# Running maxima sent as rows through DRAM, the causal mask added by GpSimd, and the gate rows turned by transposes

## The chip, the cores and the metric

The kernel runs on one core of one Trainium2 chip. A core has five engines that work side by side and meet only at semaphores: TensorE for matmuls (PE in the profile, its weight loads apart as PEld), VectorE (DVE), ScalarE (ACT), GpSimd (POOL) and SyncE (SP), which here issues every DMA from one queue, in order. Matmuls write to PSUM, eight banks of 128 x 512 floats; everything else is in SBUF, the on-chip memory with 128 partitions, or in DRAM. The metric is the device time of one execution in microseconds (us); lower is better.

## The reference, cut to what matters

The reference is one layer of a streaming encoder over 2048 tokens of 1024 features. One input projection feeds a banded attention of eight heads and an mLSTM of four heads of 128 features; gated outputs of both are projected and added to the input, and a feed-forward part of width 4096 follows, with a final norm. What the change touches is the mLSTM. For each head it has an input gate `i` and a forget gate `f` per token, both linear in the normed input, and it is computed in chunks:

```
logf = log_sigmoid(f);  bcum = cumsum(logf) within the chunk
dmat[t, s] = bcum[t] - bcum[s] + i[s]        where s <= t, else -inf
m_t = max(bcum[t] + m_st, max_s dmat[t, s])  running maximum
dw  = exp(dmat - m_t)
qk  = (q . k) * dw
num = exp(g - m_t) * (C q) + qk v;   den = exp(g - m_t) * (n . q) + sum(qk)
h   = num / max(|den|, exp(-m_t))
```

With `u[s] = i[s] - bcum[s]` and `mt` the running maximum of `u` (with the state's maximum), the weight is `dw = exp(u[s] - mt[t])`: a number per token `s`, on a partition, less a number per token `t`, along the row, and 0 where `s` is after `t`.

## The kernel before, in words

The 2048 tokens are four blocks (b = 0 to 3) of T = 512. Blocks 0 and 1 are projected one after the other with three-part matmuls (each operand is split into a rounded part and a remainder, and three products are added). Blocks 2 and 3 form a span whose products go through a scheme with seven products in place of eight over halves of the features and the two blocks: the operand list `X` holds seven sets of four tiles. Set 0 is the first half of block 2's features, set 1 its second half, set 2 the sum of both halves of block 3, set 5 the first half of block 2 less that of block 3, set 6 the second half of block 3. The feed-forward part uses the same scheme, with spans (0, 1) and (2, 3); its inner results `u` go through DRAM and come back through a ring of eight tiles.

The code is written as generators. `Flow` runs them on a clock of its own: each `yield` names an engine and a cost, gets buffers from a pool or a PSUM bank, or waits for an event. After that `Order` takes the instructions so made and lists them again for every engine by estimated lengths, transfer times and due times; the order on an engine is then fixed, and so is the one of the DMAs on SP's queue. A change in pool sizes, in costs or in instructions can thus move others too.

The mLSTM of a block runs in these steps:

- **Gate sums.** PE multiplies the gate weights `gw` (128 x 40 for each of eight feature tiles: 8 columns rounded, zeros, and at column 32 their 8 remainders) with the two parts of the normed block, 512 tokens as columns: in `dense` (L803) for blocks 0 and 1, 16 matmuls each, and in `gates_in` (L1495) for blocks 2 and 3. Block 2 takes sets 0 and 1, 16 matmuls. Block 3 takes set 0 with the first weights and set 6 with the second in one bank, and set 5 with the first weights in a second bank, 24 matmuls; the difference of the banks is its first half plus its second.
- **`gates`.** ACT copies the 40 rows (L1461), for block 3 DVE subtracts the second bank (L1464), four matmuls with a selecting matrix `sel` (L1468) put tokens on partitions and add the remainders' rows, and DVE adds the biases (block 0 scales by its norm too).
- **`gates_rest`.** A chain of small operations on 128 x 16 tiles (four chunks of 128 tokens by four heads) makes `u`, `mt` and the exponentials `ex`. At its end four transposes (L1587) bring `mt` into rows, 4 heads x 512 tokens; ACT copies them (L1589) into `mtt` and DVE writes the remainders below (L1592). Then the event `gates` is set.
- **`rec_head`**, once for each head: PE writes the mask into a bank by a bf16 matmul of an identity with `maskb` (L1670), and adds `-mt` of the head in all rows by a matmul of a selecting column of `nsel` with `mtt` (L1671). ACT takes the exponential of the four chunks with `u` as bias (L1675) into the tile `w`. PE transposes `k` (L1682) and multiplies `k` and `q` (L1693), DVE multiplies that by `w` (L1695), and the products with the values and the state follow (L1707 to L1709). Two heads at most are held at a time; `load_rec` brings their `q`, `k` and values (L1625, L1630) back from DRAM. The final transposes are L1742, and the result is stored to `mix` in DRAM and read again by `take_mix` ahead of the projection.

Weights are read into four `wraw` tiles, split by ACT (L583) and DVE (L585) into three `wsp` tiles, and used by PE. Attention (L1388, L1415, L1446) and the mLSTM of blocks 0 and 1 lie among their input projections; those of blocks 2 and 3 among the second half of the first span's feed-forward part (L644 to L646).

Of the kernel before, what the change touches and what calls it, by code (L numbers as in the profile page):

```python
# [36 lines left out]
KT = D // P  # L37
AH, AD = 8, 64
MH = 4
FF = 4096  # L40
EPS = 1e-6
NEG = -1e30
# [330 lines left out]
class Layer:  # L373
# [8 lines left out]
    def make_tiles(self, pool, psum):  # L382
        nc = self.nc
        f32 = lambda name, *shape: pool.tile([P, *shape], F32, name=name)
        f32r = lambda name, *shape: pool.tile([P, *shape], F32R, name=name)
        self.wsplit = Pool([f32r(f"wsp{i}", 2, 1024) for i in range(3)])
        self.wraw = Pool([f32(f"wraw{i}", 1024) for i in range(4)])
        self.rpool = Pool([f32r(f"r{i}", 2, T) for i in range(28)])
        self.bias = Pool([f32(f"bias{i}", 640) for i in range(2)])
        self.sc = Pool([(f32(f"sc{i}", 640), f32(f"scs{i}", 4)) for i in range(4)])  # L390
        self.temp = Pool([f32(f"tmp{i}", 516) for i in range(6)])
        self.ctx = Pool([f32(f"ctx{i}", 516) for i in range(16)])
        self.banks = Banks([psum.tile([P, 512], F32, name=f"bank{i}") for i in range(8)])
# [4 lines left out]
        self.identb = pool.tile([P, P], BF16, name="identb")  # L398
        self.maskb = pool.tile([P, 1, P], BF16, name="maskb")
        self.gw = f32r("gw", KT, 40)  # L400
        self.sel = f32("sel", 8)
# [7 lines left out]
        self.mtt = f32r("mtt", T)  # L409
        self.nsel = f32r("nsel", 8)  # L410
# [12 lines left out]
        self.fmid = [f32(f"mie{i}", NT) for i in range(NB)]  # L423
# [13 lines left out]
    def setup_late(self):  # L437
# [7 lines left out]
        zero = raw[:, 64:384]  # L445
        nc.vector.memset(zero, 0.0)
        nc.vector.tensor_copy(self.gw.rearrange("p a b -> p (a b)"), zero)
        nc.vector.tensor_copy(self.gw[:, :, 0:8], gwr)
        nc.vector.tensor_sub(self.gw[:, :, 32:40], gwr, self.gw[:, :, 0:8].bitcast(F32))
        nc.vector.memset(raw[:, :512], 0.0)  # L450
        nc.vector.tensor_copy(self.mtt, raw[:, :512])
        fl.put(self.temp, raw)
        yield "sp", 300, 2200
        nc.sync.dma_start(self.sel, io["sel"])
# [6 lines left out]
        nc.vector.tensor_copy(self.identb, self.ident)  # L461
        nc.vector.tensor_scalar(self.maskb[:, 0], self.tri, 1.0, -NEG, op0=ALU.subtract, op1=ALU.mult)
        nc.vector.tensor_scalar(self.nsel, self.sel, -1.0, None, op0=ALU.mult)
# [321 lines left out]
    def dense(self):  # L785
        fl = self.fl
        none = [None] * KT
        for b in range(2):
# [11 lines left out]
            for k in range(KT):  # L800
                yield "pe", 433
                for j in range(2):
                    self.nc.tensor.matmul(bk[:40], self.gw[:, k], vs[k][:, j],  # L803
                                          start=k == 0 and j == 0, stop=k == KT - 1 and j == 1)
# [651 lines left out]
    def gates(self, b, bk, less=None):  # L1456
        fl, nc, B, sm = self.fl, self.nc, self.blk[b], self.sm
        V = nc.vector
        (tmp,) = yield "get", self.temp, 1
        yield "act", act_ns(512, True)  # L1460
        nc.scalar.copy(tmp[:40, :512], bk[:40])  # L1461
        if less is not None:
            yield "dve", dve_ns(512)
            V.tensor_sub(tmp[:40, :512], tmp[:40, :512], less[:40])  # L1464
            fl.put(self.banks, less)
        yield "pe", 756
        for c in range(NT):
            nc.tensor.matmul(bk[:, c * 8:c * 8 + 8], tmp[:40, c * P:(c + 1) * P], self.sel[:40],  # L1468
                             start=True, stop=True)
        gf = self.gf[b % 2]  # L1470
        if b == 0:
            for c in range(NT):
                yield "dve", 85
                V.scalar_tensor_tensor(gf[:, c], bk[:, c * 8:c * 8 + 8], self.rr["x"][:, c:c + 1],
                                       self.bif[:, c], op0=ALU.mult, op1=ALU.add)
        else:
            yield "dve", 85
            V.tensor_add(gf, bk[:, :32].rearrange("p (a b) -> p a b", a=NT), self.bif)
        fl.put(self.temp, tmp)
        fl.put(self.banks, bk)  # L1480
        fl.set(B["gf"])

    def gates_in(self, A, aev):

        fl = self.fl
        for b, use in ((2, (((0, 0), (1, 4)),)), (3, (((0, 0), (6, 4)), ((5, 0),)))):
            bks = []
            for part in use:
                bks += (yield "get", self.banks, 1)
                for x, (m, k0) in enumerate(part):  # L1490
                    for k in range(4):
                        yield "wait", [aev[m][k]]
                        yield "pe", 433
                        for j in range(2):
                            self.nc.tensor.matmul(bks[-1][:40], self.gw[:, k0 + k], A[m][k][:, j],  # L1495
                                                  start=x == k == j == 0,
                                                  stop=x == len(part) - 1 and k == 3 and j == 1)
            fl.spawn(self.gates(b, *bks), 1)

    def gates_rest(self, b):  # L1500
# [84 lines left out]
        yield "pe", 428  # L1585
        for c in range(NT):
            nc.tensor.transpose(bk[:MH, c * P:(c + 1) * P], sm["mt"][:, c * MH:(c + 1) * MH], self.ident)  # L1587
        yield "act", act_ns(512, True)
        nc.scalar.copy(self.mtt[:MH], bk[:MH])  # L1589
        yield "dve", dve_ns(512)  # L1590
        yield "dve", 85
        V.tensor_sub(self.mtt[32:32 + MH], bk[:MH], self.mtt[:MH].bitcast(F32))  # L1592
        fl.put(self.banks, bk)
        fl.set(B["gates"])

    def recurrence_far(self, b):
# [3 lines left out]
        for h in range(MH):  # L1600
# [7 lines left out]
            fl.spawn(self.load_rec(b, h), 1)  # L1608
            fl.spawn(self.rec_head(b, h), 1)
# [5 lines left out]
    def load_rec(self, b, h):  # L1615
# [14 lines left out]
        fl.set(B["mvh_ev"][h])  # L1630

# [30 lines left out]
    def rec_head(self, b, h):  # L1662
# [5 lines left out]
        (bk,) = yield "get", self.banks, 1  # L1668
        yield "pe", 440
        mm(bk.rearrange("p (c t) -> p c t", c=NT), self.identb, self.maskb.to_broadcast([P, NT, P]), start=True, stop=False)  # L1670
        mm(bk, self.nsel[:, h:h + 1].to_broadcast([P, P]), self.mtt, start=False, stop=True)  # L1671
        for c in range(NT):
            n = c * MH + h
            yield "act", act_ns(128, True, 1)
            nc.scalar.activation(w[:, c * P:(c + 1) * P], bk[:, c * P:(c + 1) * P], AF.Exp,  # L1675
                                 bias=self.sm["u"][:, n:n + 1])
        fl.put(self.banks, bk)
# [9 lines left out]
        fl.put(self.banks, bk)  # L1687
        yield "wait", [B["qk_ev"][h]]
# [768 lines left out]
    def build(self):  # L2457
# [17 lines left out]
        self.rowd = {n: f32d("row" + n, T) for n in ("in1", "in2", "in3", "mid0", "mid1", "mid2", "mid3", "out0", "out1", "out2")}  # L2475
        self.wi = 0
# [17 lines left out]
        for b in range(NB):  # L2494
# [3 lines left out]
                gates=Event(), mv_slots=Event(), mv_ev=E(NT), ctx={}, mvh={}, ctx_ev=E(MH), qk_ev=E(2 * MH), og_ev=E(MH),  # L2498
# [14 lines left out]
def _layout(np, p):  # L2513
# [35 lines left out]
    x = p["x"][0]  # L2549
    eye = np.eye(P, dtype=np.float32)  # L2550
    sel = np.zeros((P, 8), np.float32)
    for j in range(8):
        sel[j, j] = sel[32 + j, j] = 1.0
# [10 lines left out]
        sel=sel,  # L2564
# [29 lines left out]
```

## Time and profile before

| | us |
|---|---|
| median of 3 runs | 2779.44 |
| lowest and highest | 2777.0 and 2782.29 |
| the profiled execution | 2782.55 |
| its span, first to last instruction | 2780.8 |

| engine | busy us | share of the span |
|---|---|---|
| PE | 2754.7 | 99% |
| DVE | 2055.0 | 74% |
| ACT | 1493.2 | 54% |
| POOL | 52.6 | 2% |

The mean granted clock of PE was 0.999 of full speed. A row of the groups reads: line, engine, operation, output and inputs, sizes, count, then busy time, mean length of one and idle time before it. Matmuls overlap, so the mean length of one is more than the step from one to the next. A row of the waits reads: who waited for whom, then us in total, times and the longest. A row of the timeline reads: start, length, and what ran. A row of the windows reads: the stretch, its length, then the busy time (and count) of PE, PEld, DVE, ACT and POOL, PE's granted clock, the busy share of the DMAs, and GB/s.

### The profile page before, as it was taken

The page shows a single profiled execution, that of the slowest core. Times are in us where ns is not written, and L with a number is a line of the kernel's source. Part 1 is how long each engine was busy: PE and PEld are TensorE (multiplying, and loading weights), DVE is VectorE, ACT ScalarE, POOL GpSimd, SP SyncE. Part 2 cuts the span into 40 slices and gives each one's busy share as a digit, 9 for nine tenths or more (in the row PEclk, how much of TensorE's full clock was granted, in tenths as well). Part 3 has the DMA queues.
Part 4 walks back from the last instruction along what each step waited for, and adds up shares of the span by engine and source line. Part 5 has one row for each costly group of instructions (what it writes and reads, how often), then busy time and mean ns, then how long its engine had stood idle before and what let it go on. Part 6 is the DMA issues. An engine that isn't in the chain of part 4 may idle for free.

```text
span 2780.8 us, 38634 instructions
## 1 busy us (share of the span) xinstructions
PE 2754.7 (99%) x13018; PEld 2288.4 (82%) x13018; DVE 2055.0 (74%) x3776; ACT 1493.2 (54%) x2608; POOL 52.6 (2%) x100
## 2 busy tenths in 40 slices
PE   9999999999999999999999999999999999999998
PEld 7888888888778888888888888888887888888887
DVE  7696789758995866886676688789888656555565
ACT  5564576544453535575556556566436655554443
POOL 0000001000000000000000000000000000000000
PEclk9999999999999999999999999999999999999999
DMA  7958759768764677588877887787877667776574
GB/s 267 294 190 283 230 164 310 248 223 314 261 206 171 235 255 257 194 273 325 288 281 269 286 245 232 231 256 255 248 251 261 208 222 263 239 238 220 190 227 151
DMA packets 329046, 678.64 MB, mean 244 GB/s; under 512 B 36840, under 2 KB 67728, under 8 KB 328848
## 3 DMA queue, kind: packets, MB, share of 16 engines
q1 hardware_dynamic: 328848, 676.18, 73.3%
q8 instruction: 102, 1.67, 0.2%
q14 instruction: 96, 0.79, 0.1%
HBM read 472.59 MB, written 203.44 MB: 243 GB/s over the span
## 4 chain that ended last, share of the span: by engine, by line
PE 88%; DVE 4%; DMA 4%; issue 2%; ACT 1%; SPq 0%; POOLq 0%; POOL 0%; DVEq 0%; ACTq 0%
PE bank L727 41%; PE bank L644 12%; PE bank L645 11%; PE bank L646 11%; PE bank L1415 2%; PE bank L1388 2%; PE bank L755 2%; PE bank L1446 2%; DVE wsp L585 1%; DMA ctx<-in_xt 1%; DMA qfar<-ctx 1%; PE bank L1707 1%; PE bank L1709 1%; PE bank L1708 1%; PE bank L1693 0%
## 5 line engine op out<-in xcount | busy, mean ns | idle before, releaser
L727 PE MATMUL bank<-r,wsp 128*128 128x512 f32 x5544 | 1266.4, 390 | 2.9 <-DVE ctx L2088 1.5
L727 PEld LDWEIGHTS bank<-r,wsp 128*128 128x128 f32 x5544 | 1037.5, 188 | 225.4 <-DVE ctx L1874 4.2
L585 DVE TENSOR_TENSOR wsp<-wraw,wsp 128x1024 fp32r<-128x1024 f32 x459 | 560.5, 1221 | 352.9 <-ACT wsp L583 343.2
L583 ACT CAST wsp<-wraw 128x1024 fp32r<-128x1024 f32 x459 | 482.1, 1051 | 449.5 <-PE bank L727 202.9
L644 PE MATMUL bank<-r,wsp 128*128 128x512 f32 x1472 | 586.0, 398 | 2.8 <-ACT r L1224 2.8
L645 PE MATMUL bank<-r,wsp 128*128 128x512 f32 x1472 | 574.8, 391 | 0.2 <-DVE r L1229 0.2
L646 PE MATMUL bank<-r,wsp 128*128 128x512 f32 x1472 | 574.8, 391 | 0.0
L646 PEld LDWEIGHTS bank<-r,wsp 128*128 128x128 f32 x1472 | 276.2, 188 | 58.8
L644 PEld LDWEIGHTS bank<-r,wsp 128*128 128x128 f32 x1472 | 276.7, 188 | 54.2 <-ACT r L1224 3.1
L645 PEld LDWEIGHTS bank<-r,wsp 128*128 128x128 f32 x1472 | 277.0, 188 | 50.5 <-DVE r L1229 0.5
L1874 DVE TENSOR_TENSOR ctx<-bank,ctx 128x512 f32<-128x512 f32 x186 | 127.0, 687 | 91.6 <-PE bank L727 91.4
L1229 DVE TENSOR_TENSOR r<-r 128x512 fp32r<-128x512 f32 x248 | 163.7, 686 | 27.3 <-ACT r L1224 26.3
L1224 ACT CAST r<-r 128x512 fp32r<-128x512 f32 x248 | 147.5, 624 | 57.1 <-DMA r<-u 53.3
L1866 ACT COPY ctx<-bank 128x512 f32<-128x512 f32 x186 | 107.8, 581 | 66.7 <-PE bank L727 65.2
L1430 ACT ACTIVATE sc<-sc,scs 128x640 f32<-128x640 f32 (+4 forms) x128 | 97.4, 762 | 73.3 <-DVE scs L1427 63.0
L2205 ACT ACTIVATE ctx<-ctx 128x512 f32<-128x512 f32 x96 | 60.6, 631 | 103.1 <-DVE ctx L1874 103.1
L1451 DVE TENSOR_TENSOR r<-bank,r 128x512 fp32r<-128x512 f32 (+1 forms) x168 | 96.9, 595 | 17.4 <-ACT r L1449 16.6
L1449 ACT CAST r<-bank 128x512 fp32r<-128x512 f32 (+1 forms) x168 | 81.5, 517 | 48.7 <-PE bank L1446 45.6
L1421 DVE CUSTOM_DVE_ANT_0 sc<-bank,bias 128x320 f32<-128x320 f32 (+3 forms) x240 | 103.4, 461 | 5.5 <-PE bank L1415 5.0
L1388 PE MATMUL bank<-r,r 128*128 128x512 f32 x336 | 95.3, 365 | 1.3 <-DVE r L1451 1.2
L602 DVE TENSOR_TENSOR wraw<-wraw,wraw 128x1024 f32<-128x1024 f32 x76 | 92.8, 1223 | 2.0
L552 DVE TENSOR_TENSOR ctx<-ctx,ctx 128x512 f32<-128x512 f32 x112 | 76.2, 686 | 13.8 <-DMA ctx<-in_wf 9.7
(258 smaller groups left out, 2721.3 us busy)
## 6 DMA issues: line engine op xcount, KB each, us to landing
wraw<-in_wf SPq DMA_DIRECT2D x178, 512.0 KB, 4.3
wraw<-wsum SPq DMA_DIRECT2D x136, 512.0 KB, 3.9
r<-u SPq DMA_DIRECT2D x224, 256.0 KB, 4.4
wraw<-in_w SPq DMA_DIRECT2D x88, 512.0 KB, 5.2
u<-ctx SPq DMA_DIRECT2D x128, 256.0 KB, 2.8
ctx<-in_wf SPq DMA_DIRECT2D x112, 256.0 KB, 4.2
wsum<-ctx SPq DMA_DIRECT2D x112, 256.0 KB, 3.8
u<-tmp SPq DMA_DIRECT2D x96, 256.0 KB, 3.5
```

The source lines that it names most:

```text
L583: nc.scalar.copy(w[:, 0], raw)
L585: nc.vector.tensor_sub(w[:, 1], raw, w[:, 0].bitcast(F32))
L644: mm(ps, lh, rh, start=first, stop=False)
L645: mm(ps, lh, rl, start=False, stop=False)
L646: mm(ps, ll, rh, start=False, stop=last)
L727: mm(ps, wv[:, x, k, n], a[:, y], start=new and k == 0 and x == y == 0, stop=k == 3 and x == 1, skip_group_check=True)
L1224: self.nc.scalar.copy(dst[:, 0], src)
L1229: self.nc.vector.tensor_sub(dst[:, 1], src, dst[:, 0].bitcast(F32))
L1388: nc.tensor.matmul(acc[:, :, c0:c0 + w], st, sl[:, :, o:o + w], start=n == 0, stop=n == total - 1)
L1421: nc.vector.tensor_tensor_reduce(out=e[:, x * w:x * w + w], in0=bks[x][:, :w], in1=br[:, j0 + x * w:j0 + x * w + w], op0=ALU.add, op1=ALU. ...
L1866: nc.scalar.copy(t[:, o:o + 512], ps)
L1874: nc.vector.tensor_add(t[:, o:o + 512], ps, t[:, o:o + 512])
```

## The change

The two matmuls and the bank at the head of `rec_head` go. `gates_rest` puts `mt` in head order, transposes it once into 16 rows of 128 (head and chunk), ACT copies them into the free one of the two `cum` tiles, and SP stores them in a DRAM tensor `rowm` of 16 x 128 for the block. For each head a new generator `row_rec` loads that head's 512 numbers from there into `w`, repeated on all 128 partitions, and POOL adds `later` (0 where the mask allows a pair, 1e30 where not), repeated over the four chunks. The exponential is now taken from `w` in place, with scale -1 and the bias `u`, and stands behind the transposes of `k`. `gw` becomes 12 tiles of 16 columns: eight rounded and eight remainders, and for four more tiles the second half's weights less the first half's. Block 3 uses set 2 with the first half's weights and set 6 with those differences, 16 matmuls in one bank. `gates` copies 16 rows and turns them by four transposes, and DVE adds the two groups of eight columns one after the other. `sel`, `nsel`, `mtt`, `identb` and `maskb` are gone, and `temp` has seven tiles for six.

```diff
-        self.temp = Pool([f32(f"tmp{i}", 516) for i in range(6)])
+        self.temp = Pool([f32(f"tmp{i}", 516) for i in range(7)])
...
-        self.gw = f32r("gw", KT, 40)
+        self.later = f32("later", 1, P)
+        self.gw = f32r("gw", KT + 4, 16)
...
+        less = raw[:, 64:96].rearrange("p (a b) -> p a b", a=4)
+        nc.vector.tensor_sub(less, gwr[:, 4:], gwr[:, :4])
...
+        nc.vector.tensor_scalar(self.later[:, 0], self.tri, NEG, -NEG, op0=ALU.mult, op1=ALU.add)
...
     def gates(self, b, bk):
-        nc.scalar.copy(tmp[:40, :512], bk[:40])
-        if less is not None:
-            V.tensor_sub(tmp[:40, :512], tmp[:40, :512], less[:40])
+        nc.scalar.copy(tmp[:16, :512], bk[:16])
         for c in range(NT):
-            nc.tensor.matmul(bk[:, c * 8:c * 8 + 8], tmp[:40, c * P:(c + 1) * P], self.sel[:40],
-                             start=True, stop=True)
+            nc.tensor.transpose(bk[:, c * 16:c * 16 + 16], tmp[:16, c * P:(c + 1) * P], self.ident[:16, :16])
...
     def gates_in(self, A, aev):
-        for b, use in ((2, (((0, 0), (1, 4)),)), (3, (((0, 0), (6, 4)), ((5, 0),)))):
+        for b, use in ((2, ((0, 0), (1, 4))), (3, ((2, 0), (6, KT)))):
...
     def gates_rest(self, b):
-        for c in range(NT):
-            nc.tensor.transpose(bk[:MH, c * P:(c + 1) * P], sm["mt"][:, c * MH:(c + 1) * MH], self.ident)
-        nc.scalar.copy(self.mtt[:MH], bk[:MH])
-        V.tensor_sub(self.mtt[32:32 + MH], bk[:MH], self.mtt[:MH].bitcast(F32))
+        V.tensor_copy(p.rearrange("p (m c) -> p m c", c=NT), v4("mt").rearrange("p c m -> p m c"))
+        nc.tensor.transpose(bk[:16, 384:512], p, self.ident)
+        nc.scalar.copy(z[:, 64:], bk[:16, 384:512])
+        nc.sync.dma_start(self.rowm[b].ap(), z[:, 64:])
...
+    def row_rec(self, b, h, w):
+        yield "wait", [B["gates"]]
+        nc.sync.dma_start(w[:, :T], bass.AP(self.rowm[b], h * T, [[0, P], [1, T]]))
+        w4 = w[:, :T].rearrange("p (c t) -> p c t", c=NT)
+        nc.gpsimd.tensor_tensor(w4, w4, self.later.to_broadcast([P, NT, P]), op=ALU.add)
+        fl.set(B["row_ev"][h])
...
     def rec_head(self, b, h):
-        (bk,) = yield "get", self.banks, 1
-        mm(bk.rearrange("p (c t) -> p c t", c=NT), self.identb, self.maskb.to_broadcast([P, NT, P]), start=True, stop=False)
-        mm(bk, self.nsel[:, h:h + 1].to_broadcast([P, P]), self.mtt, start=False, stop=True)
-            nc.scalar.activation(w[:, c * P:(c + 1) * P], bk[:, c * P:(c + 1) * P], AF.Exp,
-                                 bias=self.sm["u"][:, n:n + 1])
...
+        yield "wait", [B["row_ev"][h]]
+            nc.scalar.activation(w[:, c * P:(c + 1) * P], w[:, c * P:(c + 1) * P], AF.Exp, scale=-1.0,
+                                 bias=self.sm["u"][:, n:n + 1])
```

More of the change, by code (lines that the diff above doesn't have):

```diff
@@ L397, in make_tiles @@
         self.ones = f32("ones", 2)
-        self.identb = pool.tile([P, P], BF16, name="identb")
-        self.maskb = pool.tile([P, 1, P], BF16, name="maskb")
-        self.gw = f32r("gw", KT, 40)
-        self.sel = f32("sel", 8)
+        self.later = f32("later", 1, P)
+        self.gw = f32r("gw", KT + 4, 16)
         self.bif = f32("bif", NT, 8)
@@ L444, in setup_late @@
         yield "dve", 300
[L445 to L451, printed above, removed]
+        less = raw[:, 64:96].rearrange("p (a b) -> p a b", a=4)
+        nc.vector.tensor_sub(less, gwr[:, 4:], gwr[:, :4])
+        for to, src in ((self.gw[:, :KT], gwr), (self.gw[:, KT:], less)):
+            nc.vector.tensor_copy(to[:, :, 0:8], src)
+            nc.vector.tensor_sub(to[:, :, 8:16], src, to[:, :, 0:8].bitcast(F32))
         fl.put(self.temp, raw)
         yield "sp", 300, 2200
-        nc.sync.dma_start(self.sel, io["sel"])
         nc.sync.dma_start(self.bif[:, 0, 0:4], io["b_i"].to_broadcast([P, 4]))
@@ L1453, in turn, with gates @@
         fl.set(ev)
-    def gates(self, b, bk, less=None):
-        fl, nc, B, sm = self.fl, self.nc, self.blk[b], self.sm
+    def gates(self, b, bk):
+        fl, nc, B = self.fl, self.nc, self.blk[b]
         V = nc.vector
@@ L1460, in gates @@
         yield "act", act_ns(512, True)
-        nc.scalar.copy(tmp[:40, :512], bk[:40])
-        if less is not None:
-            yield "dve", dve_ns(512)
-            V.tensor_sub(tmp[:40, :512], tmp[:40, :512], less[:40])
-            fl.put(self.banks, less)
-        yield "pe", 756
+        nc.scalar.copy(tmp[:16, :512], bk[:16])
+        yield "pe", 440
         for c in range(NT):
-            nc.tensor.matmul(bk[:, c * 8:c * 8 + 8], tmp[:40, c * P:(c + 1) * P], self.sel[:40],
-                             start=True, stop=True)
+            nc.tensor.transpose(bk[:, c * 16:c * 16 + 16], tmp[:16, c * P:(c + 1) * P], self.ident[:16, :16])
         gf = self.gf[b % 2]
-        if b == 0:
-            for c in range(NT):
-                yield "dve", 85
[L1474 to L1478, printed above, removed]
+        for o, base in ((0, self.bif), (8, gf)):
+            if b == 0:
+                for c in range(NT):
+                    yield "dve", 85
+                    V.scalar_tensor_tensor(gf[:, c], bk[:, c * 16 + o:c * 16 + o + 8], self.rr["x"][:, c:c + 1],
+                                           base[:, c], op0=ALU.mult, op1=ALU.add)
+            else:
+                yield "dve", 85
+                V.tensor_add(gf, bk[:, :64].rearrange("p (a b) -> p a b", a=NT)[:, :, o:o + 8], base)
         fl.put(self.temp, tmp)
@@ L1485, in gates_in @@
         fl = self.fl
-        for b, use in ((2, (((0, 0), (1, 4)),)), (3, (((0, 0), (6, 4)), ((5, 0),)))):
[L1487 to L1498, printed above, removed]
+        for b, use in ((2, ((0, 0), (1, 4))), (3, ((2, 0), (6, KT)))):
+            (bk,) = yield "get", self.banks, 1
+            for m, k0 in use:
+                for k in range(4):
+                    yield "wait", [aev[m][k]]
+                    yield "pe", 433
+                    for j in range(2):
+                        self.nc.tensor.matmul(bk[:16], self.gw[:, k0 + k], A[m][k][:, j],
+                                              start=m in (0, 2) and k == j == 0, stop=k0 > 0 and k == 3 and j == 1)
+            fl.spawn(self.gates(b, bk), 1)
     def gates_rest(self, b):
@@ L1584, in gates_rest @@
         V.tensor_scalar(ex[:, 2], ex[:, 2], C1, None, op0=ALU.mult)
[L1585 to L1590, printed above, removed]
-        yield "dve", 85
-        V.tensor_sub(self.mtt[32:32 + MH], bk[:MH], self.mtt[:MH].bitcast(F32))
+        yield "dve", 85
+        V.tensor_copy(p.rearrange("p (m c) -> p m c", c=NT), v4("mt").rearrange("p c m -> p m c"))
+        yield "pe", 110
+        nc.tensor.transpose(bk[:16, 384:512], p, self.ident)
+        yield "act", act_ns(P, True)
+        nc.scalar.copy(z[:, 64:], bk[:16, 384:512])
         fl.put(self.banks, bk)
+        yield "sp", 900, 2000
+        nc.sync.dma_start(self.rowm[b].ap(), z[:, 64:])
         fl.set(B["gates"])
@@ L1608, in recurrence_far @@
             fl.spawn(self.load_rec(b, h), 1)
+            fl.spawn(self.row_rec(b, h, B["ctx"][h][3]), 1)
             fl.spawn(self.rec_head(b, h), 1)
@@ L1687, in rec_head @@
         fl.put(self.banks, bk)
+        yield "wait", [B["row_ev"][h]]
+        for c in range(NT):
+            n = c * MH + h
+            yield "act", act_ns(128, False, 1)
+            nc.scalar.activation(w[:, c * P:(c + 1) * P], w[:, c * P:(c + 1) * P], AF.Exp, scale=-1.0,
+                                 bias=self.sm["u"][:, n:n + 1])
         yield "wait", [B["qk_ev"][h]]
@@ L2475, in build @@
         self.rowd = {n: f32d("row" + n, T) for n in ("in1", "in2", "in3", "mid0", "mid1", "mid2", "mid3", "out0", "out1", "out2")}
+        self.rowm = [f32d(f"rowm{b}", 16, P) for b in range(NB)]
         self.wi = 0
@@ L2497, in build @@
                 kq_ev=E(AH), q_ev=E(AH), k_ev=E(AH), k_spilt=E(AH), kq_all=Event(), head_done=E(AH),
-                gates=Event(), mv_slots=Event(), mv_ev=E(NT), ctx={}, mvh={}, ctx_ev=E(MH), qk_ev=E(2 * MH), og_ev=E(MH),
+                gates=Event(), mv_slots=Event(), mv_ev=E(NT), ctx={}, mvh={}, ctx_ev=E(MH), qk_ev=E(2 * MH), row_ev=E(MH), og_ev=E(MH),
                 mix=[None] * 8, mix_ev=E(8), ga={}, ga_ev=E(8), xs_free=Event(), x_room=E(KT), mid=Event(), vo={}, vn={}, vp_ev=E(4), mvh_ev=E(MH), gf=Event(), rec_slots={}, heads_left=[2] * 4))
```

19 lines of the change are left out of this document (4 added, 15 removed).

## The prediction

> **What bounds the kernel now.** I read the page first, then who TensorE (PE) waited for, then the groups and order of PE's instructions around the change, and last the views of POOL and the DMAs. From the page:
>
> ```profile
> span 2780.8 us, 38634 instructions
> ...
> PE 2754.7 (99%) x13018; PEld 2288.4 (82%) x13018; DVE 2055.0 (74%) x3776; ACT 1493.2 (54%) x2608; POOL 52.6 (2%) x100
> ...
> PEclk9999999999999999999999999999999999999999
> ...
> PE 88%; DVE 4%; DMA 4%; issue 2%; ACT 1%; SPq 0%; POOLq 0%; POOL 0%; DVEq 0%; ACTq 0%
> ```
>
> PE is busy for all but 26.1 us of the span, and the chain that ended last is 88% PE. Its waits, and its busy time in the last stretch:
>
> ```profile
> PE bank L644 <- ACT r L1180: 6.7, 1, 6.7
> PE bank L644 <- ACT r L1224: 2.8, 1, 2.8
> PE bank L755 <- DVE ctx L1874: 1.6, 2, 1.3
> ...
> PE bank L1707 <- DMA r<-mvfar: 0.9, 1, 0.9
> ```
> ```profile
> 2700.00:2781.00 81.00, 71.77 (x344) 59.62 (x342) 47.54 (x66) 31.80 (x47) 2.01 (x2) 0.95 0.47 161
> ```
>
> Of the 26.1 us, 6.7 are the first wait, at the start, and 81.0 - 71.8 = 9.2 lie in the last stretch; neither place is touched. So 26.1 - 6.7 - 9.2 = 10.2 us are lost in some 2700 us between. There the next matmul is nearly always ready, and time taken from PE's stream should leave the span nearly one for one, as long as the new row path makes PE wait nowhere.
>
> A busy PE alone does not prove this. The Trainium skill (Perfetto Trace Analysis, section Identifying the Most-Contended Engine) says that matmul busy share is a bad measure of the distance from the roofline, and that the busy share of the weight loads is a good one; that is 82% here, which would leave PE headroom. That rule by itself makes the gain zero, the third rival below. The trace speaks against it where the change acts: what counts is the step from one matmul to the next, and the waits say that hardly any is lost.
>
> **The change part by part.** The PE groups that it touches, and PE's order around one pair of mask matmuls:
>
> ```profile
> L1495 PE MATMUL bank<-r,gw 128*40 128x512 f32 x40 | 9.6, 395 | 0.0
> L1671 PE MATMUL bank<-mtt,nsel 128*128 128x512 f32 x16 | 9.0, 583 | 0.0
> L1670 PE MATMUL bank<-maskb,identb 128*128 128x512 bf16 x16 | 6.2, 388 | 0.0
> L1468 PE MATMUL bank<-sel,tmp 40*128 40x8 f32 x32 | 4.2, 255 | 0.0
> L1587 PE MATMUL bank<-const,g_mt 128*4 128x128 f32 x16 | 2.4, 272 | 0.0
> ```
> ```profile
> 1837.07 0.75 PE L1415 MATMUL bank<-r,r 128*128 128x320 f32 x4
> 1837.66 0.39 PE L1670 MATMUL bank<-maskb,identb 128*128 128x512 bf16 x1
> 1837.70 0.58 PE L1671 MATMUL bank<-mtt,nsel 128*128 128x512 f32 x1
> 1838.12 0.39 PE L644 MATMUL bank<-r,wsp 128*128 128x512 f32 x1
> ```
>
> Durations overlap their neighbours, so I price by ends. The work ahead ends at 1837.07 + 0.75 = 1837.82 and L1671 ends at 1837.70 + 0.58 = 1838.28: a pair costs 0.46 us. Summing group busy times (15.2 us) would count the overlap.
>
> (1) Mask and maxima matmuls of rec_head, gone: 16 heads x 0.46 = 7.4 us.
>
> (2) Gate sums of the last block: 24 matmuls become 16, since the half sum of the span replaces two operands. The two new ones are operands already used by the quad ahead, so nothing new is awaited. A step, from the second row below: (3.91 - 0.395) / 15 = 0.234; 8 x 0.234 = 1.9 us.
>
> ```profile
> 823.72 1.05 PE L1468 MATMUL bank<-sel,tmp 40*128 40x8 f32 x8
> 824.70 3.91 PE L1495 MATMUL bank<-r,gw 128*40 128x512 f32 x16
> ```
>
> (3) The selecting matmuls of gates (two records each) become four transposes a block. Before: step (1.05 - 0.255) / 7 = 0.114, eight times 0.91 us a block. After, from below by transposes in a row, as L1587 below: (0.60 - 0.272) / 3 = 0.11 each, 0.44 a block; from above by the one transpose of 16 rows that the kernel has, L1552, none of whose 229 ns overlaps: 0.92. Four blocks save 0 to 1.9 us; I take 1.5, near the first, since they stand in a row.
>
> ```profile
> L1552 PE MATMUL bank<-const,cum x4: 229/229/229, 59.4 to 1764.7; 16*128 16x16 f32 x4
> ```
> ```profile
> 1779.94 0.60 PE L1587 MATMUL bank<-const,g_mt 128*4 128x128 f32 x4
> ...
> 1780.76 0.57 ACT L1589 CAST mtt<-bank 4x512 fp32r<-4x512 f32 x1
> 1782.21 0.68 DVE L1592 TENSOR_TENSOR mtt<-bank,mtt 4x512 fp32r<-4x512 f32 x1
> 1784.19 0.39 PE L1670 MATMUL bank<-maskb,identb 128*128 128x512 bf16 x1
> ...
> 1786.28 2.17 ACT L1675 ACTIVATE ctx<-bank,g_u 128x128 f32<-128x128 f32 x8
> ...
> 1795.67 0.68 DVE L1695 SCALAR_TENSOR_TENSOR ctx<-bank,ctx 128x512 f32<-128x512 f32 x1
> ```
>
> (4) End of gates_rest: one transpose for four, 3 x 4 blocks x 0.11 = 1.3 us of PE. ACT copies 128 columns for 512 and DVE loses the 0.68 subtraction for a small copy: off PE, taken as nothing.
>
> (5) The narrower gate weights (40 columns to 16) leave PE's step as it is, for 512 columns stream past. The setup's and gates' few DVE instructions more or less, and the second addition per block, stand far from a PE wait: nothing. Should one be late, the cost is one stall of the kind listed, 0.9 us.
>
> Sum: 7.4 + 1.9 + 1.5 + 1.3 = **12.1 us** less PE work (10.6 to 12.5 by the bounds of (3)).
>
> (6) Added: per block a store of 8 KB; per head a 256 KB load that repeats a row, an addition on POOL, and the four exponentials of L1675 reading SBUF. The nearest rows:
>
> ```profile
> tmp<-rowmid SPq DMA_DIRECT2D x8, 256.0 KB, 6.5
> ```
> ```profile
> L2127 SPq DMA_DIRECT2D mix<-ctx x16: 319/320/586, 208.6 to 1894.8; - x16
> L2189 SPq DMA_DIRECT2D r<-mix x16: 320/379/855, 434.8 to 1967.4; - x16
> ...
> DMA to landing us min/median/max: 2.0/4.1/6.1
> ```
> ```profile
> L1659 POOL TENSOR_SCALAR ctx<-ctx,ghead 128x512 f32<-128x512 f32 x8 | 12.0, 1494 | 51.8 <-ACT ctx L1656 43.5 <-issue 8.3
> ```
> ```profile
> 1470.00:1850.00 380.00, 376.89 (x1974) 319.08 (x1973) 294.19 (x727) 223.58 (x478) 12.11 (x26) 1.00 0.81 257
> ```
>
> The first head of a block now waits for: transpose 0.1, copy at most 0.57, store 4.1, row 6.5, addition 1.5 and four exponentials (2.17 / 2) 1.1, in all 13.9 us. In the last block the old transposes end at 1780.5 and the product L1695 that needs the exponentials starts at 1795.7, 15.2 us on: it comes out about even, or late by whatever the SP queue adds. On PE the score products and other work behind it stay ready. Later heads load their row beside their q, k and v, where the addition and the exponentials on ACT add up to 1.5 + 1.1 us. If all eight heads of the far half shift in turn by 2.6 us, the last head's store moves from 1894.8 by 21 us, and the last of the 16 loads of these tiles is issued at 1967.4: that cover of 72 us holds. Without it, projection would wait, for at most those 21 us.
>
> The new loads also stand in SP's queue, which is in order. The row load waits there for its store to land; behind it stand weight loads, the loads of u, and stores. The 16 rows are 4.2 MB, and the DMAs are 0.81 busy in the stretch where eight of them fall; its 257 GB/s move eight rows, 2.1 MB, in 8 us of 380, so the share goes up by about 0.02. What that costs PE is not in the trace; it is bounded by nothing below (no gain: the 10.2 us of stalls are not on the removed work) and by the one large wait of that stretch above:
>
> ```profile
> 1551.57 0.62 ACT L1224 CAST r<-r 128x512 fp32r<-128x512 f32 x1 [6.74 <-DMA r<-u]
> ...
> 1552.24 0.49 PE L644 MATMUL bank<-r,wsp 128*128 128x512 f32 x1 [2.83 <-ACT r L1224]
> ```
>
> There a load of u came late, and PE lost 2.8 us. Eight times that would be 22.6 us. I take 1 us, one wait like L1707's for its load, because PE already draws on loads of this queue at every weight tile and lost only 10.2 us. The larger temp pool (7 for 6) and the new durations make the planner write another order: the 10.2 us are drawn anew, and could be 3 or 17. I take them unchanged.
>
> Result: the profiled execution took 2782.55 us (span 2780.8 and 1.75 around it), 3.1 above the median of 2779.44. 2782.55 - 12.1 + 1 = 2771.45; by the median, 2779.44 - 11.1 = **2768.3**.
>
> **The rivals.** Slower by the queue: the row load holds up SP while its store lands, at the eight heads between 1500 and 1850 us, where a late u load reaches PE as shown. At 2.83 us each: 2779.44 - 12.1 + 22.6 = 2789.9. It decides from 12.1 / 8 = 1.5 us a head. For it: the DMAs at 0.81 and that one row. Against: eight row loads of the same form (rowmid) are in this kernel, and none appears among PE's waits.
>
> Slower by POOL and DVE: the trace has POOL and DVE in each other's way.
>
> ```profile
> 1544.86 1.23 DVE L585 TENSOR_TENSOR wsp<-wraw,wsp 128x1024 fp32r<-128x1024 f32 x1
> ```
> ```profile
> 1544.88 2.08 POOL L1729 TENSOR_TENSOR hs<-hs,half 128x4 f32<-128x4 f32 x1 [172.44 <-DVE hs L1727]
> ```
> ```profile
> L2331 POOL TENSOR_TENSOR r_z<-r_z,half 128x4 f32<-128x4 f32 x3 | 3.0, 1007 | 805.2 <-DVE r_z L2327 805.2
> ```
>
> The same POOL form takes 1.01 us at L2331; begun beside a DVE subtraction of two SBUF tiles it ends 0.9 us after that, as if it had first waited. The other way round each of the 16 additions would hold DVE for 1.5 us; if PE paid all, 24 us, and 2779.44 - 12.1 + 24 = 2791. It decides from 0.76 us per addition. Against: DVE is busy 294 of 380 us in that stretch, and the largest wait of PE for DVE in the whole list is the 1.6 us of L755. The Trainium skill (SBUF — State Buffer, section Who interferes with whom) has it as a rule: a DVE instruction with two SBUF inputs and a GpSimd one that reads SBUF exclude each other, whoever starts first. By that rule, the trace agrees (2.08 against 1.01); it does not say that PE waits.
>
> No change: the order drawn anew gives the gain back, 12.1 us of new stalls beside the old 10.2, or PE wasn't the bound: 2779. For it: the plan of before loses so little that a new one is likelier to lose more than less. Against: PE's idle list, and that the other engines have 26% (DVE) and 46% (ACT) left.
>
> **How the numbers follow.** A measurement of this kernel tells about 0.2%, 5.6 us, from no change. Forecast, 2762 to 2774: 0.72. Better still, to 2757, by fewer stalls: 0.05. No change, within 2774 to 2785: 0.12. Slower by the queue 0.07, by POOL 0.04. So faster 0.77, same 0.12, slower 0.11. The range takes in the forecast, most of the better case and the near half of no change: 2760 to 2780.
>
> **What would show it.** PE's records fall by 68 (32 mask and maxima, 8 gate sums, 16 selecting, where each had two records, and 12 transposes), its busy time by about 12 us; L1670 and L1671 are gone; 16 row loads land in about 6.5 us and 16 POOL additions take about 1.5 us; PE's waits between start and end stay near 10 us. The prediction is wrong if PE's busy time falls but r<-u or the row loads appear among PE's waits with over 6 us, or DVE's instructions beside POOL's additions lengthen and PE waits for them.

## The result and the profile after

The changed kernel takes 2787.61 us (median of 7 runs, 2784.8 to 2792.88) against 2779.44 before: a ratio of 1.0032, 95% interval 1.0022 to 1.0042. It is slower by some 8 us, where the prediction had 11 us faster. The execution profiled took 2784.80 us, the lowest of the seven, and that of before 2782.55, above its own median. So the two traces lie some 2 us apart where the medians lie 8 apart: they show what changed, but not the whole size of it.

The head of the page and of its chain, after:

```profile
span 2782.7 us, 38551 instructions
...
PE 2745.5 (99%) x12950; PEld 2284.2 (82%) x12950; DVE 2052.3 (74%) x3779; ACT 1495.2 (54%) x2608; POOL 72.5 (3%) x116
...
PE 88%; DMA 5%; DVE 3%; issue 2%; ACT 1%; SPq 0%; POOL 0%; POOLq 0%; DVEq 0%; ACTq 0%
```

PE has 68 records fewer, as forecast, and 9.2 us less busy time, yet the span is 1.9 us longer. The chain has gone from 4% DMA to 5%. The groups of PE that were changed or are new, and POOL's addition:

```profile
L1480 PE MATMUL bank<-r,gw 128*16 128x512 f32 x32 | 7.8, 395 | 0.0
L1455 PE MATMUL bank<-const,tmp 16*128 16x16 f32 x16 | 1.7, 214 | 0.1
L1572 PE MATMUL bank<-const,g_p 128*16 128x128 f32 x4 | 1.1, 271 | 0.0
L1625 POOL TENSOR_TENSOR ctx<-ctx,later 128x512 f32<-128x512 f32 x16 | 23.3, 1463 | 307.7 <-DMA ctx<-rowm 307.7
```

To see PE's work apart from its stalls, take for each kind of matmul the median step between the ends of neighbours, times its count. That sum goes from 2735.9 us to 2722.9: 12.9 us of work are gone (the sums before rounding differ by that). What PE's stream takes beyond it goes from 29.3 us to 44.5. Its waits say where:

```profile
PE bank L635 <- ACT r L1171: 6.3, 1, 6.3
PE bank L635 <- ACT r L1215: 5.8, 1, 5.8
PE bank L1668 <- DMA r<-mfar: 5.7, 3, 3.4
PE bank L746 <- DVE ctx L1866: 1.7, 2, 1.3
...
PE bank L1699 <- DVE ctx L1687: 1.4, 1, 1.4
```

The first is the start again. (The line numbers have moved: L635 was L644, L746 was L755, L1171 was L1180, L1215 was L1224, L1668 was L1682, L1685 was L1693, L1687 was L1695, L1699 was L1707.) The wait for a load of u has doubled from 2.8 us, and the transposes of k, which are now PE's first work of a head, wait 5.7 us for their loads, in three places. By stretches, before and then after:

```profile
300.00:600.00 300.00, 298.96 (x1519) 252.44 (x1517) 236.99 (x520) 184.23 (x384) 16.60 (x22) 1.00 0.71 230
1480.00:1900.00 420.00, 416.89 (x2207) 354.38 (x2206) 331.44 (x833) 246.04 (x538) 16.10 (x32) 1.00 0.82 259
```
```profile
300.00:600.00 300.00, 294.12 (x1485) 248.38 (x1484) 235.00 (x521) 181.14 (x379) 18.04 (x24) 0.99 0.69 227
1480.00:1900.00 420.00, 412.26 (x2155) 351.74 (x2154) 332.09 (x835) 245.91 (x520) 23.82 (x40) 0.99 0.82 262
```

Length less PE's busy time is its idle time: 1.0 us becomes 5.9 where block 1's heads run, and 3.1 becomes 7.7 where blocks 2 and 3 do. In both PE's clock falls to 0.99 of full speed as a mean.

At the longest wait, SP's and PE's timelines and the windows of the changed kernel:

```profile
1545.81 0.32 SPq L1622 DMA_DIRECT2D ctx<-rowm  x1
...
1547.40 3.42 SPq L2181 DMA_DIRECT2D r<-u  x4
```
```profile
1557.68 0.80 PE L635 MATMUL bank<-r,wsp 128*128 128x512 f32 x1 [5.76 <-ACT r L1215]
```
```profile
1540.00:1550.00 10.00, 10.00 (x55) 8.60 (x54) 3.68 (x9) 3.37 (x10) 0.00 (x0) 1.00 1.03 328
1550.00:1560.00 10.00, 4.24 (x20) 3.48 (x19) 3.44 (x6) 4.42 (x10) 1.26 (x1) 0.75 1.02 371
...
1555.00:1558.00 3.00, 0.32 (x1) 0.32 (x2) 0.86 (x1) 3.00 (x7) 0.00 (x0) 0.51 1.04 410
1558.00:1561.00 3.00, 3.00 (x8) 2.35 (x8) 3.00 (x7) 1.89 (x6) 0.00 (x0) 0.50 1.04 397
```

A row load stands just ahead of a weight load and the four loads of u, one of which PE then waits for by way of ACT, and the share of the DMAs (the column before the last) is 1.02 to 1.04: they are full. The mean of 0.81 over 380 us, from which the prediction added 0.02, had hidden this. After the wait PE runs at half its clock (0.51, 0.50) for some microseconds.

### The profile page after: what moved, and what is told of

The parts are those of the page before. It is cut to its first block, busy times and chain, and to the rows that moved or that the text cites. A ratio compares the mean times of both kernels' runs of the same rounds, so it can differ in the third digit from the quotient of the medians.

```text
span 2782.7 us, 38551 instructions
## 1 busy us (share of the span) xinstructions
PE 2745.5 (99%) x12950; PEld 2284.2 (82%) x12950; DVE 2052.3 (74%) x3779; ACT 1495.2 (54%) x2608; POOL 72.5 (3%) x116
## 4 chain that ended last, share of the span: by engine, by line
PE 88%; DMA 5%; DVE 3%; issue 2%; ACT 1%; SPq 0%; POOL 0%; POOLq 0%; DVEq 0%; ACTq 0%
PE bank L718 44%; PE bank L635 11%; PE bank L636 11%; PE bank L637 11%; PE bank L1406 2%; PE bank L1379 2%; PE bank L746 2%; PE bank L1437 2%; DMA ctx<-rowm 1%; DMA r<-mfar 1%; PE bank L1699 0%; DVE wsp L576 0%; DMA ctx<-in_xt 0%; PE bank L1701 0%; DMA wsum<-ctx 0%
## 5 line engine op out<-in xcount | busy, mean ns | idle before, releaser
L635 PE MATMUL bank<-r,wsp 128*128 128x512 f32 x1472 | 587.1, 399 | 5.8 <-ACT r L1215 5.8
L635 PEld LDWEIGHTS bank<-r,wsp 128*128 128x128 f32 x1472 | 277.4, 189 | 57.0 <-ACT r L1215 6.0
L1220 DVE TENSOR_TENSOR r<-r 128x512 fp32r<-128x512 f32 x248 | 165.6, 694 | 22.6 <-ACT r L1215 22.1
L1215 ACT CAST r<-r 128x512 fp32r<-128x512 f32 x248 | 148.5, 622 | 52.2 <-DMA r<-u 45.3
```

The source lines that it names most:

```text
L635: mm(ps, lh, rh, start=first, stop=False)
L1215: self.nc.scalar.copy(dst[:, 0], src)
L1220: self.nc.vector.tensor_sub(dst[:, 1], src, dst[:, 0].bitcast(F32))
```

## The experiments

Two theories stand after the result. The **row path**: the 256 KB row loads, in a DMA queue already full in places, push the loads of u and k late. The **order**: the planner writes all orders anew after any edit, and the order of before was a good draw. A third, about the **head of rec_head**: its first PE work now needs a load, where the mask matmuls needed none.

### Parts undone

**No row traffic.** The 4 stores and 16 loads are left out, and POOL fills `w` from a constant, so the weights of the pairs are not computed.

```diff
-        nc.sync.dma_start(self.rowm[b].ap(), z[:, 64:])
...
-        nc.sync.dma_start(w[:, :T], bass.AP(self.rowm[b], h * T, [[0, P], [1, T]]))
-        nc.gpsimd.tensor_tensor(w4, w4, self.later.to_broadcast([P, NT, P]), op=ALU.add)
+        lt = self.later.to_broadcast([P, NT, P])
+        nc.gpsimd.tensor_tensor(w4, lt, lt, op=ALU.add)
```

> The changed kernel without its 4 row stores and 16 row loads: POOL writes w from constants (the weights of the pairs are then wrong; all instructions of PE, ACT, DVE and POOL stay). Theory R (the row loads and stores in a DMA queue that is already full in places push the loads of k and u late): the lost time comes back, 2767 us (before less 12.9 us of PE work), stalls of PE between start and end near 10 us. Theory P (any new order of the plan draws the stalls anew, and this one was unlucky): no reason to fall below 2779; anything from 2767 to 2790. Theory K (the first PE instruction of a head now waits for a load of k, where it was a matmul that needed none): stays near 2785.

2790.81 us, ratio 1.0045 (1.0031 to 1.0059). Read alone, this speaks against the row path. But its planner saw no row loads either and wrote another order; PE's waits are at other places (first the start, then k):

```profile
PE bank L635 <- ACT r L1171: 7.1, 1, 7.1
PE bank L1665 <- DMA r<-mfar: 4.4, 2, 3.1
PE bank L1696 <- DVE ctx L1684: 3.7, 3, 2.1
...
PE bank L635 <- ACT r L1215: 1.8, 3, 1.1
```

The wait for u is down to 1.8 us and others have come. With two things changed at once, the run settles neither.

**Six temp tiles** (`range(7)` back to `range(6)`).

> The changed kernel with six temp tiles again. Theory R: no change from the changed kernel, 2784 to 2790 us. Theory P: another draw, 2770 to 2795. If the seventh tile itself is the cause, 2768 to 2772.

2794.78 us, 1.0054 (1.0037 to 1.0071). Nothing speaks for the seventh tile as the cause; but this order is a new one too, so the run does not rule it out by itself.

**The gate part alone**, on the kernel before: `gates`, `gates_in` and `gw` as changed, mask and maxima by matmuls.

> The kernel before with only the gate part of the change (narrow weights, half sum, transposes): 3 to 4 us of PE work less, no new DMA. Theories R and K: 2775 to 2777 us. Theory P: anything from 2768 to 2790, since the order is planned anew here too.

2779.74 us, 1.0003 (0.9994 to 1.0013). PE's work is 4.8 us less (2731.1 us by steps) and the time is the same, without a row load in it: above the 2775 to 2777 of theories R and K.

**The row part alone** (gates as before).

> The changed kernel with the gate part undone: rows through DRAM, POOL's addition, seven temp tiles. Theories R and K: slower than the changed kernel by its 3 to 4 us of PE work, 2788 to 2792 us. Theory P: anything from 2772 to 2795.

2792.57 us, 1.0043 (1.0028 to 1.0059), with the wait of 5.8 us for u at the same place. It fits theory P, and R and K as well within the noise (0.6 us above their range).

### The order drawn anew

One constant of the planner, `Flow.SLACK = 800.0`, is set to another value. The kernel computes the same with the same instructions; their order differs, and with it which buffers they use.

> The kernel before, the same instructions, only the planner's SLACK constant at 820 ns for 800, so that it writes another order. Theory P (a new order draws the stalls anew, and the order of before is a good draw): slower than 2779 by 3 to 15 us. Theory K (the stalls come from the head of each mLSTM head, where PE's first instruction now waits for k): within 4 us of 2779.

> The same with 780 ns: a second draw. Theory P: 2782 to 2795 us. Theory K: within 4 us of 2779.

> The changed kernel, SLACK at 900 ns: the same instructions in another order. Theory P: another draw about a mean near 2780 to 2790. Theory K: stays at 2784 to 2792, with PE waits for r<-mfar of over 3 us again.

The kernel before takes 2789.12 us with 820 (1.0026, 1.0015 to 1.0037) and 2794.43 with 780 (1.0051, 1.0034 to 1.0069); the changed one takes 2787.08 with 900 (1.0022, 1.0012 to 1.0032), the same as with 800, with waits of 5.7 us for k and 5.3 us for u. So the order alone is worth as much as the whole result. PE's waits and the stretch of block 1's heads with 780, where there is neither a row load nor any other part of the change:

```profile
PE bank L1682 <- DMA r<-mfar: 4.8, 3, 2.5
PE bank L644 <- ACT r L1224: 2.9, 1, 2.9
```
```profile
300.00:600.00 300.00, 294.47 (x1486) 248.37 (x1486) 233.28 (x517) 181.57 (x379) 15.11 (x21) 0.99 0.68 222
```

The wait for k is there too, so it isn't owed to the removed mask matmuls; and 5.5 us are idle where the order of before has 1.0. The wait for u is 2.9 us as before.

**The transposes of k behind the exponentials**, in the order in which the changed `rec_head` is written.

> The changed kernel with the transposes of k put behind the exponentials in the order in which the head is written, as they stood before. Theory K: PE's waits for r<-mfar (5.7 us in the changed kernel) fall to under 1 us and the time to about 2778. Theory P: another draw, the sum of waits about as before, 2780 to 2792.

2794.98 us, 1.0051 (1.0036 to 1.0065); PE still waits 5.0 us for k. The head theory falls. (The time is above the range of theory P too.)

### The same order, smaller rows

To part the row path from the order, the rows were made small without a change of order: one partition is loaded in place of 128, the planner still reckons the transfer at its full size, and POOL writes `w` from constants behind the load (so the weights of the pairs are again not computed). The orders on PE, DVE, ACT and SP are those of the changed kernel.

```diff
-        nc.sync.dma_start(w[:, :T], bass.AP(self.rowm[b], h * T, [[0, P], [1, T]]))
+        nc.sync.dma_start(w[:1, :T], bass.AP(self.rowm[b], h * T, [[0, 1], [1, T]]))
...
```

> The changed kernel with every row load cut from 256 KB to one partition's 2 KB, and POOL writing w from constants after it (the weights of the pairs are then wrong). The orders on PE, DVE, ACT and SP are those of the changed kernel, instruction for instruction. If the bytes of the rows cause the wait of 5.8 us for a load of u at 1552 us (the theory of the row path, held to that place), it falls to 3 us or less, its slow clock goes, and the time is 2780 to 2783 us. If the order alone makes the stalls, they stay, and the time is 2786 to 2789.

2778.31 us, 1.0006 (0.9997 to 1.0015): 9.3 us less than with full rows, and a little below the range that was expected. The constants in `w` are not what makes it faster: the run without row traffic has them too and took 2790.81. PE's waits, its timeline at the old place, and the stretches:

```profile
PE bank L1668 <- DMA r<-mfar: 7.5, 3, 4.3
...
PE bank L635 <- ACT r L1215: 1.7, 1, 1.7
```
```profile
1553.78 1.20 PE L635 MATMUL bank<-r,wsp 128*128 128x512 f32 x4 [1.66 <-ACT r L1215]
```
```profile
300.00:600.00 300.00, 296.15 (x1507) 250.53 (x1506) 238.30 (x529) 184.38 (x386) 17.73 (x24) 0.99 0.70 229
1480.00:1900.00 420.00, 418.20 (x2196) 356.40 (x2195) 341.94 (x858) 250.78 (x533) 21.28 (x40) 1.00 0.82 260
```

The wait at 1552 us is 1.7 us for 5.8, PE's idle time from 1480 to 1900 us is 1.8 us for 7.7, and the clock there stays whole. The wait for k does not fall, it grows from 5.7 to 7.5 us: it belongs to the order, not to the bytes. While the full row lands, the DMAs also move less; the same three microseconds with the full row, then with the small one:

```profile
1549.00:1552.00 3.00, 2.92 (x19) 2.42 (x17) 1.39 (x2) 0.13 (x2) 0.00 (x0) 1.00 0.94 243
```
```profile
1549.00:1552.00 3.00, 3.00 (x19) 2.59 (x18) 2.10 (x2) 1.34 (x6) 1.17 (x1) 1.00 1.03 386
```

243 GB/s against 386: at this place the load holds the others up by more than its own 256 KB. Why is not shown.

Three more runs repeat the comparison in other orders, and draw the kernel before a third time:

> The order of the changed kernel with SLACK at 900 (which took 2787.1 us), rows cut to 2 KB as in the run before with tiny rows; instruction for instruction the same. If the bytes of the rows cost about 9 us whatever the order: 2776 to 2780 us. If they cost it only in one order: 2784 or more.

> The changed kernel in a third order (SLACK 780). If orders drawn anew scatter about the changed kernel: 2783 to 2795 us.

> That third order with tiny rows: the second pair. 7 to 11 us less than its full rows if the bytes cost the same everywhere, 0 to 4 us less if not.

> The kernel before in a third order of its own (SLACK 700), the same instructions. If the order of before is a good draw and others cost 9 to 14 us, 2785 to 2795 us; if those two were bad draws, 2776 to 2782.

| order | full rows | small rows | difference |
|---|---|---|---|
| SLACK 800 | 2787.61 | 2778.31 | 9.3 |
| SLACK 900 | 2787.08 | 2774.82 | 12.3 |
| SLACK 780 | 2787.16 | 2775.96 | 11.2 |

With 900 and 780 the kernel with small rows is faster than before: 0.9982 (0.9973 to 0.9990) and 0.9981 (0.9972 to 0.9989). The full rows with 780 are at 1.0026 (1.0016 to 1.0035). The stretch from 1480 to 1900 us with full rows, then with small ones, both with 780:

```profile
1480.00:1900.00 420.00, 411.50 (x2144) 349.96 (x2143) 330.24 (x830) 245.77 (x520) 22.96 (x40) 0.99 0.84 261
```
```profile
1480.00:1900.00 420.00, 418.98 (x2201) 357.09 (x2200) 343.07 (x860) 252.31 (x537) 21.24 (x40) 1.00 0.83 260
```

8.5 us of idle time against 1.0. PE's wait for u falls from 5.3 to 2.6 us with 900, and from 4.5 to 0.3 with 780. Both differences are a little above what was expected. The third draw of the kernel before takes 2786.78 us, 1.0021 (1.0012 to 1.0029).

### Trying to mend it

The planner was told that a load is 2.5 us later for a PE instruction that reads it directly, and its margin for loads, so far kept for the other engines, now counts for PE too. Some 240 of PE's 12950 instructions then stand at another place.

```diff
-                at[j] = max(at[j], r)
+                at[j] = max(at[j], r + (2500.0 if e == "SP" and to == "PE" else 0.0))
-                safe[j] = max(safe[j], r + (self.MARGIN[e] if to != "PE" and (to != e or e == "SP") else 0.0))
+                safe[j] = max(safe[j], r + (self.MARGIN[e] if (to != "PE" or e == "SP") and (to != e or e == "SP") else 0.0))
```

> The changed kernel, with the planner taking a load to be 2.5 us later for a PE instruction that reads it directly; PE's order differs in a few places only. If PE's waits for r<-mfar come from an order written for loads that land early, they fall from 5.7 us to under 2, and the time by 4 to 7 us, to 2780 to 2784. If not, 2786 to 2790.

> The same edit of the planner in the kernel before, which waits for loads on PE for 0.9 us in all. Nothing to gain: 2777 to 2782 us if a small change of order is harmless; above 2784 if any change of its order costs stalls.

The changed kernel then takes 2792.21 us (1.0046, 1.0033 to 1.0060), the kernel before 2779.76 (1.0000, 0.9991 to 1.0008). In the first, the wait has in part moved to the products of k and q (L1685), which read loads of mfar too:

```profile
PE bank L1685 <- DMA r<-mfar: 4.1, 1, 4.1
...
PE bank L1668 <- DMA r<-mfar: 3.5, 2, 2.3
```

So it is not mended by placing PE's instruction later alone. The same edit with the gate part alone, in three orders:

> The gate part alone with the same edit of the planner: 4.8 us of PE work less than before, no rows. 2773 to 2778 us if its waits for loads go; 2779 or more if the order drawn anew eats the gain again.

> The gate part alone with the later loads in the planner (2776.9 us) in another order, SLACK 820. If that order was a good draw as the one of before is, 2783 to 2792 us; if the edit makes the orders good, 2773 to 2778.

> The same with SLACK 760: a second draw, by the same two readings 2783 to 2792 or 2773 to 2778 us.

2776.89 us (0.9993, 0.9985 to 1.0002), 2780.34 (0.9999, 0.9990 to 1.0008) and 2789.86 (1.0036, 1.0022 to 1.0049): one in each of the two ranges and one between them, so the edit does not make orders good. No version that computes the whole reference is shown to be faster than before; the first of these three comes nearest.

## Why the prediction was wrong

**The PE work was right.** 12.1 us were forecast, 12.9 measured by steps. By the same steps terms (1), (2) and (4) come to 7.4, 1.9 and 1.3 us, as forecast. In (3) the busy time of the group fell from 4.2 to 1.7 us, 2.5 us, where 1.5 was taken and 1.9 was the upper end. The step of 0.11 was read off L1587, a transpose of another shape; the new ones are quicker:

```profile
829.48 0.42 PE L1455 MATMUL bank<-const,tmp 16*128 16x16 f32 x4
```

The last of the four takes 0.21, so a step is (0.42 - 0.21) / 3 = 0.07 us.

**Term (6) was mis-sized.** "I take 1 us" for the row path; it costs 9.3, 12.3 and 11.2 us in three orders, 10.9 as a mean, for identical orders on PE, DVE, ACT and SP. Its own upper bound was 22.6. The reasons given for the low end failed. The share of the DMAs was read as a mean over 380 us (0.81); over ten microseconds at the place of the longest wait it is 1.02 to 1.03. In the profile of before that could be seen as well:

```profile
1510.00:1520.00 10.00, 10.00 (x49) 8.27 (x47) 4.81 (x6) 7.04 (x10) 0.00 (x0) 1.00 1.05 327
1520.00:1530.00 10.00, 10.00 (x48) 8.31 (x47) 3.73 (x6) 5.49 (x10) 0.00 (x0) 1.00 0.99 292
1530.00:1540.00 10.00, 10.00 (x57) 8.63 (x57) 4.59 (x8) 2.59 (x7) 0.00 (x0) 1.00 1.03 300
1540.00:1550.00 10.00, 9.41 (x46) 7.60 (x44) 4.02 (x12) 2.48 (x7) 2.08 (x1) 1.00 0.95 308
```

The eight rowmid loads, named as evidence against, do not overlap that stretch: they begin later than 1600 us. The rival "slower by the queue" named the outcome, a late load of u that reaches PE, with a chance of 0.07, but not the way to it. It had SP held while the row store lands; in the changed kernel none of SP's waits for that store is over 0.9 us, and the small rows keep the store, the wait for it and the order, without the cost. Nor was it eight waits of 2.8 us each, but mainly one wait that is 5.8 us with full rows and 1.7 with small ones, smaller ones, and the slow clock behind them. The runs with small rows leave the bytes and the 128 packets of a row load together; which of the two it is was not tried.

**"The 10.2 us are drawn anew ... I take them unchanged" failed by as much again.** Three draws of the kernel before take 2789.1, 2794.4 and 2786.8 us, 7.3 to 15.0 above it, 10.7 as a mean (7.1 to 14.2, 10.1 as a mean, above the executions of the kernel before that were timed beside each). The prediction gave the reason itself ("the plan of before loses so little that a new one is likelier to lose more than less"), but spent it on the rival without a change and not on its sum. The terms as measured: 2779.4 - 12.9 of PE work + 10.9 for the rows + 10.7 for the order = 2788.1, against 2787.6. The last term is a mean over three draws that lie 7.6 us apart, so its part is known to a few microseconds only. The runs with small rows bear it out from the other side: they are 11.8, 8.3 and 9.4 us above 2779.4 - 12.9 = 2766.5. Whether all of that is the order, or in part something else of the change such as POOL's additions, is not shown. What in the planner makes the order of before better stays open.

**The waits of the heads** for their rows were thought to stay off PE's path, and nearly do. ACT waits for POOL's additions 27.6 us in all, and at one place that reaches PE: a row lands late, POOL, ACT and DVE (which multiplies by `w`) follow, and PE loses 1.6 us.

```profile
218.54 1.29 POOL L1625 TENSOR_TENSOR ctx<-ctx,later 128x512 f32<-128x512 f32 x1 [1.74 <-DMA ctx<-rowm]
```
```profile
219.86 1.28 ACT L1678 ACTIVATE ctx<-ctx,g_u 128x128 f32<-128x128 f32 x4 [2.47 <-POOL ctx L1625]
```
```profile
221.23 0.69 DVE L1687 SCALAR_TENSOR_TENSOR ctx<-bank,ctx 128x512 f32<-128x512 f32 x1 [2.95 <-ACT ctx L1678]
```
```profile
221.98 0.50 PE L635 MATMUL bank<-wsp,r 128*128 128x512 f32 x1 [1.59 <-DVE ctx L1687]
```

That row loads take 6.5 us and POOL's additions 1.5 was right (6.5 and 1.46).

**The POOL rival did not decide.** The exclusion itself is there: beside an addition of POOL a DVE subtraction that takes 0.69 us just before takes 1.49.

```profile
1500.21 0.69 DVE L1220 TENSOR_TENSOR r<-r 128x512 fp32r<-128x512 f32 x1
1501.11 1.49 DVE L1220 TENSOR_TENSOR r<-r 128x512 fp32r<-128x512 f32 x1 [0.21 <-ACT r L1215]
```
```profile
1500.37 1.69 POOL L1625 TENSOR_TENSOR ctx<-ctx,later 128x512 f32<-128x512 f32 x1 [125.34 <-DMA ctx<-rowm]
```

Over all 16 additions, the DVE instructions beside them take 2.2 us longer than the median of their kind, and PE waits for none of these. In other orders it is more, 8.6 us with SLACK 900; but the runs with small rows keep the additions, lose 6.3 to 8.4 us of DVE's time beside them, and are 9 to 12 us faster than their full rows. So this is not what the rows cost. By the rule of the Trainium skill that the prediction named (SBUF — State Buffer, section Who interferes with whom) a DVE instruction with two inputs in SBUF has to wait for a GpSimd one that reads SBUF and began first; the trace agrees.

**"PE was not the bound"** finds no support. The three draws with small rows take 2776.4 us as a mean, the three draws of the kernel before 2790.1: 13.7 us apart, where PE's work is 12.9 less. The draws scatter by 3.5 and 7.6 us, so this is no exact test. The 82% of the weight loads, which seemed to leave room, are what a full stream shows here: a load takes 0.188 us (L727, as a mean) and the step of its matmuls is 0.227, which makes 83%.

## What to carry to other kernels

Where the order of the work is written by a planner, time the same instructions in a few other orders before a gain of half a per cent is credited to a change, or a loss blamed on it: here the order alone moved the same kernel by 7 to 15 us. To price a transfer, keep the order fixed and shrink the transfer. And read the share of the DMAs in windows of about ten microseconds, not over the whole stage alone: here 0.82 over 420 us hid stretches that were full.

## What was not expected of the hardware

A wait on PE can cost more than its length. After 5.8 us of idle time PE's clock was 0.50 to 0.51 of full speed in the windows shown, and after 3.4 us (at 455 to 458 us) it was 0.50 too:

```profile
461.00:464.00 3.00, 2.52 (x12) 2.25 (x12) 2.02 (x6) 1.39 (x5) 0.00 (x0) 0.50 1.04 414
```

After the 2.8 us wait of the kernel before, at 1549 us, it stayed at 1.00:

```profile
1550.00:1560.00 10.00, 7.53 (x33) 5.98 (x34) 7.42 (x11) 4.30 (x7) 0.00 (x0) 1.00 1.05 394
```

The length of the wait alone does not decide. With the gate part alone the clock is 0.50 behind a wait of 1.9 us (at 1547 us); with small rows and SLACK 780 it is 1.00 behind one of 3.0 us (at 223 us):

```profile
1548.61 0.50 PE L644 MATMUL bank<-r,wsp 128*128 128x512 f32 x1 [1.90 <-ACT r L1224]
```
```profile
1550.50:1553.50 3.00, 3.00 (x9) 2.32 (x8) 3.00 (x6) 0.56 (x2) 0.00 (x0) 0.50 1.04 395
```
```profile
226.21 0.66 PE L1668 MATMUL bank<-const,r 128*128 128x128 f32 x4 [3.02 <-DMA r<-mfar]
```
```profile
226.00:229.00 3.00, 2.79 (x16) 2.42 (x16) 0.66 (x3) 1.77 (x8) 1.04 (x1) 1.00 0.92 264
```

The Trainium skill (TensorE: Matmul & The Clock Gate, section Part 1: The HAM clock gate) says that the clock is halved after an idle window of about 3.4 us. The waits of 5.8, 3.4, 3.0 and 2.8 us agree; the one of 1.9 us does not, and there the measurement decides. What else goes into it stays open. So a load that comes a few microseconds later than it did can turn a wait without aftermath into one with a slow clock behind it.
